# Moving tiles of a fused encoder layer by 32 bytes in SBUF

## The chip, the cores and the metric

The kernel runs on one core of a Trainium2 chip, in one launch. The metric is device microseconds of that core, from the first to the last instruction of the program; the figure that counts is the median of several runs.

## The reference

One layer of a bidirectional encoder over 512 tokens of width 2048, with 16 learned tokens put in front. All operands are float32.

```python
hn = rmsnorm(h, pre_norm_g)                       # h: 16 + 512 tokens
proj = hn @ w_in                                  # split into qa ka va ga qb kb vb gb
# mixer A: 8 query heads of 128, 2 key/value heads, norm and axial rotary on q and k
ya = softmax(qa @ ka.T / sqrt(128)) @ va * silu(ga)
# mixer B: 8 heads; two score maps of 64 with a distance penalty
a = softmax(s1 + bias) - lam * softmax(s2 + bias)
yb = rmsnorm(a @ vb, subln_g) * (1 - lambda_init) * silu(gb)
y = concat(ya, yb) @ w_out
out = h + rmsnorm(y, post_norm_g)                 # the 512 real tokens
```

## The kernel before, in words

Every large product is made on TensorE from float32r operands. Each operand is split into a high part (ScalarE, `hi`, or the activation of L154 and L179) and the rest (VectorE, `lo`, L155 and L180), and three products are accumulated in PSUM: high x high, low x high and high x low. So every logical matmul is a triple of instructions, each with its own load of the held operand ("LDWEIGHTS") and its own stream. `Lanes.mm` (L63) and `Lanes.transpose` (L66) record all of them, so their line is that of the helper; the tile names tell them apart.

Which operand is held and which is streamed differs:
- `three` (in `dense_T`, and in the first stage, a loop over 16 slices k of the width): the weights `wh`, `wl` are held, 128 columns each, and the tokens `xh[k]`, `xl[k]` are streamed. The tiles of tokens have 528 columns (16 learned, 512 real). For keys and values (`KEYS`) they are streamed in two halves of 264 columns, for queries and gates (`REAL`) as one slice of 512 columns that begins 16 columns, 64 bytes, into the tile.
- `queries_A`: the tokens are held, in slices of 128, and the weights are streamed, 512 columns.
- `dense_out` and `product(of_y(...))`: the gated heads `oh[j]`, `ol[j]` are held, in slices of 128, and the output weights are streamed, 512 columns.
- `product(of_t(...))`: sums of gated heads, `u` and `v`, are held, in slices of 128, and sums of output weights are streamed, 512 columns. `dense_out` makes the first and the fourth column block of the output; the two blocks between take seven smaller products in place of eight: two with `of_y`, two with `of_t`, one with `of_y`, two with `of_t`.
- `transpose`: the tile is held and the identity `ident` is streamed, 128 columns.

The stages: up to some 75 us the tokens are loaded and the first head's projections are made; then the eight heads of mixer B, each with its projections; from about 500 us mixer A, with its queries in two groups (`queries_A`) and a gate per head; from about 750 us the output product. The order of TensorE's work is fixed when the program is made: `lanes` runs the dense products in a loop and, after each triple, lets waiting tasks (scores, transposes, probability times values, norms) put in a few instructions of theirs when a clock that adds up nominal durations has passed their due time. Weights come through a ring of three buffers (`wp`) on the SP queue, 512 KB at a time.

Tiles take their places from pools, one after the other in the order of their first use, each rounded up to 32 bytes in a partition. The pools `cst`, `wp`, then `ap` (later `yp`) grow from the low end. The pools `xp` (tokens) and, after it is given back, `op` (gated heads) lie against the high end, which is byte 229,344 of a partition. So, in bytes of a partition before the change:
- `xp`: `xh0` begins at 161,760 = 64 x 2,527 + 32, and the 32 tiles of 2,112 bytes (64 x 33) that follow each other all begin 32 past a multiple of 64;
- `op`: `oh0` begins at 163,808 = 64 x 2,559 + 32, and the 32 tiles of 2,048 bytes likewise;
- `ident` begins at 17,824 = 64 x 278 + 32, `rB` behind it at 18,336 = 64 x 286 + 32;
- `wh`, `wl`, and the large tiles of `ap` and `yp` (among them `u`, `v`, `ph`, `pl`, `vh`, `vl`, `p`, the scores' operands) begin at multiples of 64, and `ones_r` does.

Of the kernel before, what the change touches and what calls it, by code (L numbers as in the profile page):

```python
# [10 lines left out]
F32 = mybir.dt.float32  # L11
# [6 lines left out]
P = 128  # L18
# [90 lines left out]
def kernel(ctx: ExitStack, tc: tile.TileContext, xT, xn, xm, w_s, w_t, w_q, w_o,  # L109
# [7 lines left out]
    cst = ctx.enter_context(tc.tile_pool(name="cst", bufs=1))  # L117
# [5 lines left out]
    xp = xst.enter_context(tc.tile_pool(name="xp", bufs=1, side="right"))  # L123
# [7 lines left out]
    def ctile(shape, name, dt=F32, src=None, pool=cst):  # L131
        t = pool.tile(shape, dt, name=name, tag=name, bufs=1)
        if src is not None:
            load(t, src)
        return t

    def load(out, in_):

        tc.keep_in_program_order(nc.sync.dma_start(out=out, in_=in_))
# [32 lines left out]
    nc.scalar.dma_start(out=gcol, in_=gpre)  # L172
    xh = [xp.tile([P, NT], F32R, name=f"xh{k}", tag=f"xh{k}") for k in range(KT)]
    xl = [xp.tile([P, NT], F32R, name=f"xl{k}", tag=f"xl{k}") for k in range(KT)]

    def xload(k):
        st = ap.tile([P, NT], F32, name="xs", tag="p", bufs=6)
        load(st, xT[k])
        nc.scalar.activation(xh[k], st, AF.Identity, scale=gcol[:, k:k + 1])  # L179
        nc.vector.scalar_tensor_tensor(out=xl[k], in0=st, scalar=gcol[:, k:k + 1],  # L180
                                       in1=xh[k].bitcast(F32), op0=ALU.mult, op1=ALU.subtract)
# [38 lines left out]
    for k0 in range(0, KT, 2):  # L220
        xload(k0)
        wh, wl = wload(w_s[k0 // 2], 768, load, 2 if k0 == 0 else 1)
        xload(k0 + 1)
        for k in (k0, k0 + 1):
            for i, (segs, pss) in enumerate(zip(start, first)):
                c = slice((i + 3 * (k - k0)) * P, (i + 3 * (k - k0) + 1) * P)
                for (n0, n1), ps in zip(segs, pss):
                    three(ps[:, :n1 - n0], wh[:, c], wl[:, c], k, n0, n1)
# [8 lines left out]
    def rstd(dst, ss, n, rows=P):  # L237

        nc.gpsimd.tensor_scalar(out=dst, in0=ss, scalar1=1.0 / n, scalar2=EPS,
                                op0=ALU.mult, op1=ALU.add)  # L240
        nc.gpsimd.tensor_tensor(out=dst, in0=dst, in1=mhalf[:rows, :dst.shape[1]], op=ALU.pow)  # L241
# [18 lines left out]
    nc.vector.tensor_tensor(out=rm, in0=ssm[:, 0:1], in1=ssm[:, 1:2], op=ALU.add)  # L260
    rstd(rt, rt, DM)
    rstd(rm, rm, DM, NM)
    ident = ctile([P, P], "ident", src=ident_d)
    rB = ctile([P, NT], "rB")
    dg = ap.tile([P, NT], F32, name="dg", tag="tT")
# [14 lines left out]
    sinT = ctile([P, TT, P], "sinT", src=sin_d, pool=ap)  # L280
    gqB = ctile([P, P], "gqB", src=gq, pool=ap)
    gkB = ctile([P, P], "gkB", src=gk, pool=ap)
    sgc = ctile([P, 1], "sgc", src=gsub)
    nc.vector.tensor_scalar(out=sgc, in0=sgc, scalar1=1.0 - LAMBDA_INIT, scalar2=None,
                            op0=ALU.mult)
# [19 lines left out]
    def hi(dst, src):  # L305
        nc.scalar.activation(dst, src, AF.Copy)  # L306

    def lo(dst, src, h):
        nc.vector.tensor_tensor(out=dst, in0=src, in1=h.bitcast(F32), op=ALU.subtract)  # L309
# [446 lines left out]
    op = ctx.enter_context(tc.tile_pool(name="op", bufs=1, side="right", reuse_waits="tile"))  # L756
    oh = [op.tile([P, SEQ], F32R, name=f"oh{j}", tag=f"oh{j}") for j in range(KT)]
    ol = [op.tile([P, SEQ], F32R, name=f"ol{j}", tag=f"ol{j}") for j in range(KT)]
    for j in range(0, KT - 4, 2):
        st = wp.tile([P, 1024], F32, name="os", tag="st")  # L760
        nc.sync.dma_start(out=st.rearrange("p (i q) -> p i q", i=2),
                          in_=oscr[j // 2].rearrange("i p q -> p i q"))
        for i in range(2):
            hi(oh[j + i], st[:, i * SEQ:(i + 1) * SEQ])
            lo(ol[j + i], st[:, i * SEQ:(i + 1) * SEQ], oh[j + i])
# [273 lines left out]
```

## Time and profile before

| what | value |
|---|---|
| runs | 954.44, 956.00, 956.57 us |
| median | 956.0 us |
| span of the profiled execution | 953.9 us; the page has no other time of it |
| mean granted TensorE clock | 0.990 |
| PE busy | 926.4 us, 97% |
| DVE, ACT, POOL busy | 584.6, 482.0, 164.0 us |
| data moved | 117.16 MB, mean 123 GB/s |

PE is TensorE's matmuls, PEld its loads of held operands, DVE VectorE, ACT ScalarE, POOL GpSimd, SP the engine whose queue issues most transfers. In a row of the groups stand: line, engine, operation, output <- inputs by the program's names (for a matmul the streamed operand first, then the held one: `pd<-xh,wh` streams `xh` past held `wh`), the shape, the count, the busy time and mean ns of one, and the idle time before. A matmul's recorded duration overlaps the next one's; the distance between the starts of two is what one costs. In a row of the windows stand: the stretch in us from the span's start, its length, each engine's busy time and the count of its instructions that were under way in it, the granted clock as a share of the full one, the mean share in which the transfer engines were busy, and GB/s. A row of the timeline gives start, duration, engine, line and operation; a row of the chain gives start, duration and what the end waited for.

### The profile page before, as it was taken

The numbers are of one execution on the slowest core, as the hardware profiler recorded it, in microseconds if no ns is written. First come the engines' busy times: TensorE is split into PE (matmuls) and PEld (weight loads), VectorE is DVE, ScalarE is ACT, GpSimd is POOL, SyncE is SP. The second block draws the span as 40 slices with busy tenths as digits, with TensorE's granted clock in tenths as the row PEclk, the third lists the DMA queues.
The fourth block names the chain that finished last, engine by engine and source line by source line (L and its number), as shares of the span: only waits on it lengthen the run. The fifth ranks groups of instructions, "written<-read, shape, count | busy, mean of one in ns | idle before, by whom it ended". The sixth has DMA issues, their size and how long they took to land.

```text
span 953.9 us, 14190 instructions
## 1 busy us (share of the span) xinstructions
PE 926.4 (97%) x5498; PEld 810.8 (85%) x5498; DVE 584.6 (61%) x974; ACT 482.0 (51%) x845; POOL 164.0 (17%) x250
## 2 busy tenths in 40 slices
PE   9999999999999999999999999998999999999983
PEld 8899898989989898998997888886888888888862
DVE  6386576757575574757554274447554662476996
ACT  6664655546464554746552254354555743245531
POOL 0001010101001010101201041226212123201054
PEclk9999999999999999999999999999999999999996
DMA  9742122222223222312223223211222346976785
GB/s 333 260 159 99 67 88 88 79 77 100 76 78 99 82 84 77 100 67 78 89 67 100 89 68 109 67 58 54 80 75 78 128 141 202 292 226 193 232 278 196
DMA packets 40611, 117.16 MB, mean 123 GB/s; under 512 B 4672, under 2 KB 9536, under 8 KB 40416
## 3 DMA queue, kind: packets, MB, share of 16 engines
q1 hardware_dynamic: 37072, 104.71, 33.2%
q0 software_dynamic: 3328, 11.54, 4.1%
q8 instruction: 43, 0.70, 0.3%
q14 instruction: 24, 0.20, 0.1%
q10 hardware_dynamic: 144, 0.01, 0.0%
HBM read 107.85 MB, written 8.39 MB: 122 GB/s over the span
## 4 chain that ended last, share of the span: by engine, by line
PE 84%; DVE 7%; DMA 2%; POOL 2%; ACT 2%; issue 1%; SPq 0%; DVEq 0%; POOLq 0%; ACTq 0%
PE pd L63 54%; PE po L63 14%; PE sc L63 6%; PE pv L63 5%; PE tr L66 5%; DVE wl L155 1%; DVE qn L578 1%; DMA st<-in_w_o_dram 1%; DVE y L939 1%; POOL qn L592 1%; DMA ch<-in_w_o_dram 1%; POOL ssh L241 1%; DMA xns<-in_xn_dram 1%; DMA xs<-in_xT_dram 1%; ACT qn L650 0%
## 5 line engine op out<-in xcount | busy, mean ns | idle before, releaser
L63 PE MATMUL pd<-xh,wh 128*128 128x264 f32 (+1 forms) x992 | 333.3, 336 | 0.0
L63 PE MATMUL pd<-xl,wh 128*128 128x264 f32 (+1 forms) x992 | 324.9, 327 | 0.4 <-DVE xl L180 0.4
L63 PE MATMUL pd<-xh,wl 128*128 128x264 f32 (+1 forms) x992 | 324.9, 328 | 0.4 <-DVE wl L155 0.4
L154 ACT ACTIVATE wh<-st 128x1024 fp32r<-128x1024 f32 (+2 forms) x135 | 139.8, 1038 | 208.3 <-PE pd L63 90.5
L155 DVE TENSOR_TENSOR wl<-st,wh 128x1024 fp32r<-128x1024 f32 (+2 forms) x135 | 161.7, 1198 | 98.9 <-ACT wh L154 97.7
L63 PEld LDWEIGHTS pd<-xh,wl 128*128 128x128 f32 x992 | 186.6, 188 | 17.8 <-DVE wl L155 0.7
L63 PEld LDWEIGHTS pd<-xh,wh 128*128 128x128 f32 x992 | 187.3, 189 | 12.9 <-ACT xh L179 0.2
L63 PEld LDWEIGHTS pd<-xl,wh 128*128 128x128 f32 x992 | 187.5, 189 | 12.0 <-DVE xl L180 0.6
L63 PE MATMUL po<-wh,ol 128*128 128x512 f32 x176 | 69.6, 396 | 0.9 <-DVE ol L309 0.9
L63 PE MATMUL po<-wh,oh 128*128 128x512 f32 x176 | 70.3, 400 | 0.0
L63 PE MATMUL po<-wl,oh 128*128 128x512 f32 x176 | 69.8, 397 | 0.0
L463 ACT ACTIVATE p<-p,mx 128x528 f32<-128x528 f32 x64 | 46.5, 728 | 34.2 <-POOL mx L460 34.0
L453 DVE CUSTOM_DVE_ANT_0 p<-sc,dist 128x528 f32<-128x528 f32 x64 | 44.9, 702 | 24.0 <-PE sc L63 23.5
L309 DVE TENSOR_TENSOR pl<-tr,ph 128x512 fp32r<-128x512 f32 x64 | 43.4, 688 | 16.2 <-ACT ph L306 15.0
L306 ACT ACTIVATE ph<-tr 128x512 fp32r<-128x512 f32 x64 | 37.6, 590 | 30.9 <-PE tr L66 30.6
L63 PE MATMUL pd<-wh,xh 128*128 128x512 f32 x128 | 52.2, 408 | 0.8 <-DVE vf L300 0.8
L66 PE MATMUL tr<-ident,p 128*128 128x128 f32 (+1 forms) x320 | 50.9, 273 | 1.7 <-DVE gA L558 0.9
L63 PE MATMUL pd<-wh,xl 128*128 128x512 f32 x128 | 50.6, 395 | 0.0
L63 PE MATMUL pd<-wl,xh 128*128 128x512 f32 x128 | 50.5, 395 | 0.0
L66 PEld LDWEIGHTS tr<-ident,p 128*128 128x128 f32 (+1 forms) x320 | 37.3, 132 | 13.4 <-DVE gA L558 1.6
L413 POOL TENSOR_SCALAR pm<-pm 32x256 fp32r<-32x256 f32 x32 | 20.1, 627 | 149.7 <-ACT pm L306 145.8
L460 POOL TENSOR_SCALAR mx<-mx 128x2 f32<-128x2 f32 x32 | 12.1, 377 | 196.0 <-DVE mx L453 196.0
(206 smaller groups left out, 1582.6 us busy)
## 6 DMA issues: line engine op xcount, KB each, us to landing
st<-in_w_t_dram SPq DMA_DIRECT2D x82, 512.0 KB, 3.6
st<-in_w_o_dram SPq DMA_DIRECT2D x40, 512.0 KB, 4.3
st<-in_w_q_dram SPq DMA_DIRECT2D x16, 512.0 KB, 3.6
xs<-in_xT_dram SPq DMA_DIRECT2D x16, 264.0 KB, 5.7
xns<-in_xn_dram SPq DMA_DIRECT2D x8, 512.0 KB, 5.3
ch<-in_w_o_dram POOLq DMA_DIRECT2D x8, 512.0 KB, 8.8
out_dram<-y SPq DMA_DIRECT2D x16, 256.0 KB, 2.3
os<-oscr SPq DMA_DIRECT2D x6, 512.0 KB, 3.6
```

The lines of the kernel that those rows point to most:

```text
L63: self._add(self.nc.tensor.matmul(out, lhsT, rhs, start=start, stop=stop), us)
L66: self._add(self.nc.tensor.transpose(out, in_, ident), 0.109)
L154: nc.scalar.activation(wh[:, c], st[:, c], AF.Copy)
L155: nc.vector.tensor_tensor(out=wl[:, c], in0=st[:, c], in1=wh[:, c].bitcast(F32), op=ALU.subtract)
L241: nc.gpsimd.tensor_tensor(out=dst, in0=dst, in1=mhalf[:rows, :dst.shape[1]], op=ALU.pow)
L306: nc.scalar.activation(dst, src, AF.Copy)
L309: nc.vector.tensor_tensor(out=dst, in0=src, in1=h.bitcast(F32), op=ALU.subtract)
L413: nc.gpsimd.tensor_scalar(out=pm[32:64], in0=pm[0:32].bitcast(F32), scalar1=1.0, scalar2=1.0, op0=ALU.mult, op1=ALU.mult)
L453: nc.vector.tensor_tensor_reduce(out=two(p), in0=sc[:, :, :HALF], in1=two(dist[:, w0:w0 + NT]), scale=1.0, scalar=-3.0e38, op0=ALU.add, op ...
L460: nc.gpsimd.tensor_scalar(out=mx, in0=mx, scalar1=-0.125, scalar2=1.0, op0=ALU.mult, op1=ALU.mult)
L463: nc.scalar.activation(p2[m], p2[m], AF.Exp, scale=0.125, bias=mx[:, m:m + 1], accum_out=sm[:, m:m + 1])
L578: nc.vector.scalar_tensor_tensor(out=raw[:, i, :], in0=raw[:, i, :], scalar=ss[:rows, i:i + 1], in1=g[:rows], op0=ALU.mult, op1=ALU.mult)
```

## The change

A helper `pad` takes a tile of 8 columns, 32 bytes in a partition, that nothing reads or writes. It is called four times: at the end of `xp`, at the end of `op`, ahead of `ident`, and ahead of `sgc` (behind `rB`). No instruction is added, taken away or moved in order; only addresses differ.

From the sizes: `xp` and `op` grow by 32 bytes and begin 32 bytes lower, `xh0` at 161,728 = 64 x 2,527 and `oh0` at 163,776 = 64 x 2,559, and all their tiles with them begin at multiples of 64. `ident` begins at 17,856 = 64 x 279 and `rB` at 18,368 = 64 x 287. The third pad brings what follows to 64 bytes further up than before: `wp`, `ap` and `yp` move by 64 bytes and keep their places in 64.

```diff
+    def pad(pool, name):
+
+        pool.tile([P, 8], F32, name=name, tag=name, bufs=1)
+
...
     xh = [xp.tile([P, NT], F32R, name=f"xh{k}", tag=f"xh{k}") for k in range(KT)]
     xl = [xp.tile([P, NT], F32R, name=f"xl{k}", tag=f"xl{k}") for k in range(KT)]
+    pad(xp, "xpad")
...
+    pad(cst, "ipad")
     ident = ctile([P, P], "ident", src=ident_d)
     rB = ctile([P, NT], "rB")
...
     gkB = ctile([P, P], "gkB", src=gk, pool=ap)
+    pad(cst, "spad")
     sgc = ctile([P, 1], "sgc", src=gsub)
...
     oh = [op.tile([P, SEQ], F32R, name=f"oh{j}", tag=f"oh{j}") for j in range(KT)]
     ol = [op.tile([P, SEQ], F32R, name=f"ol{j}", tag=f"ol{j}") for j in range(KT)]
+    pad(op, "opad")
```

## The prediction

> **What bounds the kernel now.** I read the page first, its engine shares and the chain that ended last.
>
> ```profile
> span 953.9 us, 14190 instructions
> PE 926.4 (97%) x5498; PEld 810.8 (85%) x5498; DVE 584.6 (61%) x974; ACT 482.0 (51%) x845; POOL 164.0 (17%) x250
> PEclk9999999999999999999999999999999999999996
> PE 84%; DVE 7%; DMA 2%; POOL 2%; ACT 2%; issue 1%; SPq 0%; DVEq 0%; POOLq 0%; ACTq 0%
> PE pd L63 54%; PE po L63 14%; PE sc L63 6%; PE pv L63 5%; PE tr L66 5%; DVE wl L155 1%; DVE qn L578 1%; DMA st<-in_w_o_dram 1%; DVE y L939 1%; POOL qn L592 1%; DMA ch<-in_w_o_dram 1%; POOL ssh L241 1%; DMA xns<-in_xn_dram 1%; DMA xs<-in_xT_dram 1%; ACT qn L650 0%
> ```
>
> TensorE sets the time: 84% of the chain is matmuls, and those that read xh, xl (pd) or oh, ol (po) are 68% of the span. Nothing is removed or added, so the only thing that can change is the pace of a matmul whose operands move. A "busy" matmul here overlaps the next one, so I don't use mean durations; I use the distance between starts. Next come the groups by shape, for the counts.
>
> ```profile
> L63 PE MATMUL pd<-xh,wh 128*128 128x264 f32 x608 | 177.1, 291 | 0.0
> L63 PE MATMUL pd<-xh,wh 128*128 128x512 f32 x384 | 156.2, 407 | 0.0
> L63 PE MATMUL po<-wh,oh 128*128 128x512 f32 x176 | 70.3, 400 | 0.0
> L63 PE MATMUL pd<-wh,xh 128*128 128x512 f32 x128 | 52.2, 408 | 0.8 <-DVE vf L300 0.8
> L66 PE MATMUL tr<-ident,p 128*128 128x128 f32 x256 | 38.5, 273 | 1.7 <-DVE gA L558 0.9 <-DVE pl L309 0.8
> L63 PE MATMUL po<-wh,uh 128*128 128x512 f32 x32 | 12.5, 391 | 0.0
> ```
>
> The first operand named is the one that streams, the second the one held in the array. Each row has two sisters (three products per tile), so 3 x (384 + 176 + 128) = 2064 matmuls of 512 columns have exactly one operand that now starts 32 bytes past a multiple of 64: the streamed xh or xl slice (1152), the held oh or ol slice (528), the held xh or xl slice (384). The 512-column matmuls on u and v in the last stage have none: both operands start at multiples of 64 today. They are the comparison that the trace offers. The windows below each hold one kind alone: the product of oh and ol with the fourth weight block, u and v, the y product between u and v (again oh, ol), and the first queries of mixer A with two gates.
>
> ```profile
> 803.20:852.43 49.23, 49.23 (x212) 1.00 0.91 279
> 878.77:898.72 19.95, 19.95 (x89) 1.00 0.61 189
> 899.19:909.69 10.50, 10.50 (x46) 1.00 0.90 305
> 517.34:573.32 55.98, 55.98 (x241) 1.00 0.27 82
> ```
>
> The count takes in the one matmul that was under way at the left edge. So the spacing is 49.23/211 = 233.3 ns with oh, 19.95/88 = 226.7 ns with u and v, 10.50/45 = 233.3 ns with oh again, and 55.98/240 = 233.3 ns with xh, at full clock in all four. The same three values of 233.3 and the one of 226.7 stand under DMA shares from 0.27 to 0.91, so DMA load doesn't make the difference; the second and third windows adjoin. The start times show that this is a steady beat, not a mean over accidents:
>
> ```profile
> 896.91 0.39 PE L63 MATMUL po<-wh,vh 128*128 128x512 f32 x1
> 897.14 0.39 PE L63 MATMUL po<-wh,vl 128*128 128x512 f32 x1
> 897.36 0.39 PE L63 MATMUL po<-wl,vh 128*128 128x512 f32 x1
> 897.59 0.39 PE L63 MATMUL po<-wh,vh 128*128 128x512 f32 x1
> ...
> 899.66 0.39 PE L63 MATMUL po<-wh,oh 128*128 128x512 f32 x1
> 899.89 0.40 PE L63 MATMUL po<-wh,ol 128*128 128x512 f32 x1
> 900.13 0.39 PE L63 MATMUL po<-wl,oh 128*128 128x512 f32 x1
> 900.36 0.39 PE L63 MATMUL po<-wh,oh 128*128 128x512 f32 x1
> ```
>
> Three products take 0.68 us with v and 0.70 us with oh. 6.6 to 6.7 ns a matmul is the price that I attach to an operand that starts off a multiple of 64; 2064 of them would be 13.8 us.
>
> **What of it is really had: the settling time.** The fast beat isn't there at once. After a wait at 913.4 the u products start again:
>
> ```profile
> 913.72:916.05 2.33, 2.33 (x12) 1.00 0.78 283
> 916.05:918.54 2.49, 2.49 (x12) 1.00 0.56 197
> 910.16:912.24 2.08, 2.08 (x11) 1.00 0.93 295
> 204.48:208.44 3.96, 3.96 (x19) 1.00 0.25 88
> 211.38:215.58 4.20, 4.20 (x21) 1.00 0.22 68
> ```
>
> The first ten starts after the wait are 2.33/10 = 233 ns apart (two in flight at the left edge), the next eleven 2.49/11 = 226.4. So even with both operands aligned about ten matmuls pass at the slow pace after a wait. After the change from oh to u at 910, without a wait, nine take 2.08 us, 231 each (the third row), before 227 comes; at the change at 877 four do. I take seven. A run of 512-column matmuls shorter than that gains nothing. The last two rows are runs in a head of mixer B: 17 matmuls in 3.96 us and 18 in 4.20, 233 each, between score and value products that break them off (the counts have those in flight at the edges).
>
> **The change part by part.**
> - xh and xl (tiles of tokens) as streamed operand, 512 columns. 96 lie in the first stage, in runs of six between 264-column ones: nothing. In mixer B 14 projections x 48 = 672: the head from 200 to 256 us has 96 in runs of 17, 18, 17 and 12 and shorter ones; less seven each the four leave 36 of 96, so 252 of 672 gain, 1.7 us. Of the gates of mixer A (384) two stand in the window at 517 and are counted there; the other 288, the queries outside that window (240) and most of the first output block (some 150) run between attention steps: of their runs, hardly longer than a dozen, I take one in eight, 85 matmuls, 0.6 us.
> - xh and xl as held operand, with those two gates: the unbroken run at 517 to 573, 240 - 7 = 233 x 6.67 = 1.6 us. The chain goes through it, and the wait for the normalised queries behind it starts from its end, so it moves along.
> - oh and ol (gated heads) as held operand, from 800 to 877 us: 329 matmuls without a break, 322 x 6.67 = 2.1 us. The 48 of the y product at 899 would save 0.3 us, but the chain has left TensorE by 902:
>
> ```profile
> 800.32:877.16 76.84, 76.84 (x330) 1.00 0.81 245
> ...
> 902.19 1.22 DVE wl L155
> ...
> 905.78 5.10 DMA ch<-in_w_o_dram
> ...
> 922.69 8.85 DMA st<-in_w_o_dram
> ```
>
>   VectorE and two weight transfers carry the last 40 us; I count those 48 at nothing. In the 49 us from 803 the transfers run at a share of 0.91, and weights that come late there could eat up to 1 us of the 2.1; that stays in the range.
> - xh and xl streamed at 264 columns (3 x 608 and 96 into sc). 264 columns are 1056 bytes, 16 and a half times 64. Today the first half of the keys starts at an odd 32 and the second at a multiple of 64; afterwards it is the other way round, so one half of each pair starts well either way. The rows are, first half, second half, first half again:
>
> ```profile
> 112.34 0.28 PE L63 MATMUL pd<-xh,wh 128*128 128x264 f32 x1
> 112.71 0.28 PE L63 MATMUL pd<-xh,wh 128*128 128x264 f32 x1
> 113.07 0.29 PE L63 MATMUL pd<-xh,wh 128*128 128x264 f32 x1
> ...
> 115.24 0.29 PE L63 MATMUL sc<-s,q 128*128 128x264 f32 x1
> ```
>
>   Three products take 0.37 and 0.36 us by turns, and the two only change places: nothing.
> - The identity as streamed operand of the transposes. Four take 0.44 us in the chain, 110 ns each, for a quarter of the columns that take 227 to 233: something other than the stream, most likely the load of the held operand, sets their pace, and that operand doesn't move relative to 64. I take nothing. From above, 6.67 ns for each of some 400 would be 2.7 us; from below a loss would need them to lie on the stream, which the aligned start excludes.
>
> ```profile
> 743.23 0.44 PE tr L66 x4
> ```
>
> - rB, and the instructions of VectorE and ScalarE that write xh, xl, oh, ol: off the chain, DVE 61% and ACT 51% busy; nothing. All tiles after the third pad move by 64 bytes, so none changes its place in 64.
>
> Sum: 1.7 + 0.6 + 1.6 + 2.1 = 6.0 us, made against the profiled 953.9 us, which is 2.1 us under the median of 956.0; I subtract it from the median: 950.0. With ten matmuls to settle it is about 5, with four 7.5.
>
> **Rivals.**
> 1. No settling cost where the run starts without a wait: all 2064 gain but the 48, 13.4 us, 942.6. For it: the switch at 877 settled in four. Against: nine at 910, ten after each wait.
> 2. Only the held operand counts. The comparison at 898 shows the held operand alone; that a streamed xh costs the same is read from 233.3 in its runs, without an aligned partner. Then the out stage (2.1) and the 144 of the window at 517 that aren't gates (0.9) remain: 953.0.
> 3. The start isn't the cause, and nothing moves: 956.0. u and v also lie in another region than oh and ol. The two products of 512 columns on ones_r, with both operands at multiples of 64, take 0.24 and 0.23 us:
>
> ```profile
> 118.62 0.40 PE L63 MATMUL ss<-sh,ones_r 128*128 128x512 f32 x1
> 118.86 0.39 PE L63 MATMUL ss<-sl,ones_r 128*128 128x512 f32 x1
> 119.09 0.28 PE L63 MATMUL pd<-xh,wh 128*128 128x264 f32 x1
> ```
>
>   I put that down to settling; it is also what a wrong cause looks like. [...]
> 4. Slower. What counts is the place in 128, not 64. Today weights and u, v start 64 past a multiple of 128; the 64 bytes of shift put them on multiples of 128, while xh and oh come to 64 past one. If the beat wants the present place, the narrow matmuls (1920 keys, 448 scores, 416 values) could each lose the same 6.67 ns: 18.6 us against the sum's 6.0, so 968.6. It decides once over 900 of the 2,784 lose it. Nothing in the trace shows such a place; nothing excludes it.
>
> [...]
>
> **How the numbers follow.** The sum 0.60; rival 1 0.10; rival 2 0.08; rival 3 0.14; rival 4 0.08. The first three are faster by over 0.2% (1.9 us, about what a measurement tells from no change): 0.78. Same 0.14, slower 0.08. The range goes from rival 1, 942.0, to 955.0, which leaves out rival 4 and most of rival 3; the likeliest case alone lies from 948.5 to 952.0, by settling times from four to ten and 1 us of late weights.
>
> **What would show it.** The products of oh and ol from 800 us at 226.7 ns a matmul; the run at 517 the same; in mixer B runs that begin at 233 and end at 227; transposes at 110 and 264-column matmuls at 121 as before; the last 50 us unchanged in length. Wrong would be: 233.3 in the unbroken runs (rival 3), 226.7 at once everywhere (rival 1), 264-column matmuls beyond 121 (rival 4), or new waits for weights in the out stage.

## The result, and the profile after

| | before | changed |
|---|---|---|
| median, runs side by side | 956.25 us (954.40 to 956.87, 10 runs) | 953.76 us (952.49 to 955.52, 10 runs) |
| ratio, with 95% interval | | 0.9981 [0.9972, 0.9990] |
| span of the profiled execution | 953.9 us | 952.0 us |
| mean granted TensorE clock | 0.990 | 0.991 |

The medians differ by 2.5 us; the ratio, 0.9981, stands for 1.8 us (1.0 to 2.7). The forecast was 6.0. Two rows of the page after the change:

```profile
span 952.0 us, 14190 instructions
PE 926.1 (97%) x5498; PEld 811.3 (85%) x5498; DVE 584.9 (61%) x974; ACT 481.6 (51%) x845; POOL 162.8 (17%) x250
```

The instructions are the same, in the same order, and TensorE is busy for 926.1 us as against 926.4. The 13.8 us that the prediction could have had at most are nowhere. The windows that answer to those of before hold oh and ol with the fourth weight block, u and v, the y product between, and the first queries of mixer A (stretch, length, then PE, PEld, DVE, ACT and POOL each with its count, then clock, DMA share, GB/s):

```profile
803.31:852.30 48.99, 48.99 (x211) 39.27 (x210) 25.05 (x33) 16.60 (x26) 9.14 (x13) 1.00 0.91 277
879.21:897.79 18.58, 18.58 (x83) 15.40 (x82) 18.58 (x19) 12.25 (x17) 3.57 (x2) 1.00 0.65 197
899.64:909.43 9.79, 9.79 (x43) 7.89 (x42) 9.52 (x11) 3.29 (x4) 0.58 (x1) 1.00 0.89 306
517.38:572.37 54.99, 54.99 (x239) 44.72 (x238) 23.38 (x37) 19.39 (x48) 10.71 (x12) 1.00 0.27 79
```

The count again takes in one matmul under way at the left edge. The spacing is 48.99/210 = 233.3 ns with oh, 18.58/82 = 226.6 with u and v, 9.79/42 = 233.1 with oh again: all as before, although oh and ol now begin at multiples of 64. The queries alone are faster, 54.99/238 = 231.1 against 233.3. The 233.3 in the unbroken runs is the sign which the prediction named as wrong. But 231.1 is no pace: it is a mixture. The queries take twelve matmuls for each token slice k, and the start times of the changed kernel's matmuls show another pace for each k:

```profile
533.09 0.39 PE L63 MATMUL pd<-wl,xh 128*128 128x512 f32 x1
...
535.38 0.39 PE L63 MATMUL pd<-wh,xh 128*128 128x512 f32 x1
...
536.08 0.39 PE L63 MATMUL pd<-wh,xh 128*128 128x512 f32 x1
...
538.12 0.40 PE L63 MATMUL pd<-wh,xh 128*128 128x512 f32 x1
...
540.68 0.39 PE L63 MATMUL pd<-wl,xh 128*128 128x512 f32 x1
```

From the first row to the second lie ten matmuls on k = 9, 2.29 us, 229.0 each. From the third to the fourth lie nine on k = 10, 2.04 us, 226.7. From the fourth to the fifth lie eleven on k = 11, 2.56 us, 232.7. All these slices start at multiples of 64. What tells them apart is their place in 256 bytes: a token tile is 2,112 bytes, 64 more than a multiple of 256, so the slice moves on by 64 from one k to the next while the weights stay. Counted as held start less streamed start, modulo 256, the distance is 192 at k = 9, 0 at k = 10, 64 at k = 11. In the out stage it is 64 for oh and 0 for u and v; before, it was 160 for oh, 0 for u and v, and an odd multiple of 32 for every token slice.

Since the order is the same (in e6 but for three), the matmuls of two traces can be matched one to one. The table shows by how much TensorE of each kernel is ahead of the kernel before; e1 to e6 are the kernels of the experiments below (us, by the start of the matmul that begins at the given time before; the last column is the span):

| kernel | 76 | 502 | 578 | 754 | 804 | 915 | last | span |
|---|---|---|---|---|---|---|---|---|
| changed | 0.0 | 0.2 | 0.6 | 1.2 | 0.6 | 0.4 | 1.2 | 1.9 |
| oh as weights (e1) | -0.1 | 0.1 | 0.5 | 0.9 | 1.0 | 3.6 | 1.0 | 2.1 |
| all at odd 32 (e3) | 0.7 | 1.2 | 1.6 | 2.7 | 2.7 | 2.9 | 3.5 | 3.4 |
| tokens as weights (e4) | 0.9 | 2.8 | 3.8 | 4.7 | 4.8 | 5.0 | 5.3 | 5.9 |
| the same, 32 off (e4c) | -0.2 | 0.2 | 0.2 | 0.6 | 0.6 | 0.6 | 1.4 | 2.1 |
| tokens and oh (e5) | 0.2 | 2.0 | 3.1 | 4.6 | 4.3 | 5.4 | 5.6 | 5.2 |
| and residual moved (e6) | 0.0 | 1.8 | 2.9 | 3.9 | 4.2 | 4.2 | 10.0 | 5.4 |

Up to 76 us the chain of the kernel before has two loads in it (`xs`, 4.79 us from 2.11, and `xns`, 4.86 from 38.25), and one execution differs from the next there by several tenths: e4 and e5 have the same addresses up to there and differ by 0.6; e2, not in the table, is 1.4 behind at 76.

### The profile page after: what moved, and what is told of

It reads as the page before. It is cut to its first block, busy times and chain, and to the rows that moved or that the text cites. A ratio compares the mean times of both kernels' runs of the same rounds, so it can differ in the third digit from the quotient of the medians.

```text
span 952.0 us, 14190 instructions
## 1 busy us (share of the span) xinstructions
PE 926.1 (97%) x5498; PEld 811.3 (85%) x5498; DVE 584.9 (61%) x974; ACT 481.6 (51%) x845; POOL 162.8 (17%) x250
## 4 chain that ended last, share of the span: by engine, by line
PE 77%; DMA 7%; DVE 7%; ACT 3%; POOL 3%; issue 2%; DVEq 0%; POOLq 0%; ACTq 0%
PE pd L63 55%; PE po L63 8%; PE sc L63 5%; PE tr L66 5%; PE pv L63 4%; DMA ts<-oscr 3%; DMA ch<-in_w_o_dram 2%; DVE qn L585 1%; DVE wl L159 1%; DVE y L947 1%; DMA st<-in_w_o_dram 1%; POOL qn L599 1%; DMA os<-oscr 1%; POOL ssh L246 1%; ACT oh L313 0%
## 5 line engine op out<-in xcount | busy, mean ns | idle before, releaser
L557 ACT ACTIVATE p<-sc,mxA 128x528 f32<-128x528 f32 x32 | 22.4, 700 | 44.6 <-POOL mxA L554 44.5
```

Source lines behind the costliest of these rows:

```text
L557: nc.scalar.activation(two(p), sc[:, :, :HALF], AF.Exp, scale=ASCALE, bias=mx, accum_out=sm)
```

## The experiments

The runs are named m1, e1 and so on; each ratio is against the kernel before, run beside that kernel. Three theories stood after this. S, the prediction's: each operand's own start in 64 bytes sets the pace. R: the region sets it (u and v lie elsewhere than oh). D: the distance between the held and the streamed start, modulo 256, sets it.

**The pair alone (m1).** A small kernel on zeros that leaves the layer out: 24 matmuls per case, held slices at a chosen distance from the streamed ones.

```
h = (m + d) // 4 + (i % 4) * P          # held: start m + d bytes, slices 512 bytes apart
s = m // 4 + (i % 2) * 1024             # streamed: start m bytes
mm(ps[:, :n], held[:, h:h + P], moved[:, s:s + n], ...)
```

> Only matmuls on zeros, none of the layer: for each case 24 matmuls that alternate over two streamed slices, with held slices at a set distance in bytes from the streamed ones. Theory D (the distance between held and streamed start, modulo 256, sets the beat; in the trace after, the queries with xh at distance 0 run at 226.7 ns, at 192 at 228.6, all others at 232 to 235): 512 columns at distance 0 and at 256 and 512 take 226 to 227 ns, whether the streamed slice starts at 0 or 32 past; 64 and 128 take 232 to 234 in both; 320 as 64. Theory S (each operand's own start in 64 bytes sets it, as predicted): all distances that are multiples of 64 run alike at 226.7 with start 0, and all cases with start 32 at 233 or more. Theory R (the region of SBUF in which the tiles lie sets it): no case differs from another of its width. For 264 and 256 columns D expects the same order of distances with 1 to 3 ns between best and worst, around 121 and 118 ns; S and R none.

Each row of the timeline is one case, named by its streamed columns, the streamed start m and the distance d. The next row's start less its own, over 24, is the spacing.

```profile
22.99 5.60 PE L36 MATMUL c512m0d0z<-moved,held 128*128 128x512 f32 x24
28.43 5.61 PE L36 MATMUL c512m0d16z<-moved,held 128*128 128x512 f32 x24
33.88 5.75 PE L36 MATMUL c512m0d32z<-moved,held 128*128 128x512 f32 x24
39.47 5.76 PE L36 MATMUL c512m0d48z<-moved,held 128*128 128x512 f32 x24
...
89.75 5.66 PE L36 MATMUL c512m0d192z<-moved,held 128*128 128x512 f32 x24
95.25 5.76 PE L36 MATMUL c512m0d208z<-moved,held 128*128 128x512 f32 x24
...
111.91 5.63 PE L36 MATMUL c512m32d0z<-moved,held 128*128 128x512 f32 x24
117.37 5.76 PE L36 MATMUL c512m32d64z<-moved,held 128*128 128x512 f32 x24
122.97 5.67 PE L36 MATMUL c512m32d192z<-moved,held 128*128 128x512 f32 x24
128.48 5.62 PE L36 MATMUL c512m0d256z<-moved,held 128*128 128x512 f32 x24
133.93 5.76 PE L36 MATMUL c512m0d320z<-moved,held 128*128 128x512 f32 x24
139.53 5.63 PE L36 MATMUL c512m0d512z<-moved,held 128*128 128x512 f32 x24
```

Distance 0 gives (28.43 - 22.99)/24 = 226.7 ns, 16 gives 227.1, 32 gives 232.9, 192 gives 229.2. With both starts moved by 32 the distances 0 and 64 give 227.5 and 233.3, and 256 and 320 give 227.1 and 233.3 like 0 and 64. Over the last twelve of each case, when the beat is steady, 0, 16, 240, 256 and 512 have 226.67, 192 has 228.9, 176 has 230.0, and all others lie between 232.1 and 234.3. Starts at an odd 32 do no harm here if both are so (227.5 at distance 0); starts at multiples of 64 don't help if they are 64 apart (232.9). S falls, and R too, since both tiles stay where they are; D stands for 512 columns. With 264 columns the steady spacing is 120.0 to 123.3; with 256 columns it is 117.1 to 120.0, and distance 0 is among the slowest, against D's expectation.

**oh and ol to the place of the weights (e1), u and v away from it (e2).** On the changed kernel; room comes from writing `lpr` in place.

```diff
-    lpr = ctile([P, 2, 64], "lpr")
+    lpr = lmt[:, 0::2, :]
+    pad(cst, "lowpad", 256)
-    pad(op, "opad")
+    pad(op, "opad", 96)          # e1
+    pad(yp, "ypad", 64)          # e2, ahead of the chain's tiles
```

> The changed kernel with the gated heads 64 bytes lower, so that held oh and ol and streamed wh and wl start at the same place modulo 256 (128 and 128); the low pools move by 256 bytes, lpr is written in place. Theory D: the unbroken products of oh and ol from 800 us on go from 233.3 to 226.7 ns a matmul, the queries and gates of mixer A stay at 231 to 232 in the mean; 329 x 6.7 = 2.2 us less by 877 us, 1.5 to 2.5 us off the changed kernel's time, so 0.995 to 0.997 of the kernel before. Theory S: both start at multiples of 64 already, 233.3 as in the changed kernel, no change against it (0.998). Theory R: oh and ol stay in the same region, 233.3, no change.

> The changed kernel with 64 bytes of padding ahead of the tiles of the output stage, so that held u and v lie 64 bytes past the streamed weights modulo 256; all still start at multiples of 64. Theory D: the products of u and v slow from 226.7 to 233.3 ns; the 94 ahead of the y product take 0.6 us more, the end 0 to 1 us later because VectorE carries it. Theories S and R: u and v stay at 226.7.

e1 took 953.40 us, a ratio of 0.9974 [0.9963, 0.9984], an interval that overlaps the changed kernel's: the 1.5 to 2.5 us that were expected don't show in the time. e2 took 954.74 in one run; it is read for its paces only, as are the other single runs (e3, e4c). The windows of e1 (oh; u and v) and of e2 (the same):

```profile
803.34:852.29 48.95, 48.95 (x217) 40.55 (x216) 26.69 (x35) 18.34 (x30) 8.71 (x12) 1.00 0.88 276
880.01:897.90 17.89, 17.89 (x80) 14.82 (x79) 17.72 (x19) 10.62 (x14) 0.00 (x0) 1.00 0.69 217
```

```profile
803.40:852.39 48.99, 48.99 (x211) 39.27 (x210) 25.16 (x34) 16.57 (x25) 9.31 (x14) 1.00 0.91 279
879.70:898.35 18.65, 18.65 (x81) 14.96 (x80) 18.65 (x19) 12.24 (x17) 3.01 (x2) 1.00 0.63 196
```

With oh at the weights' place its products take 48.95/216 = 226.6 ns; with u and v off it theirs take 18.65/80 = 233.1. Either pace was switched by addresses alone. From 804 to 877 us, where oh and ol run alone, TensorE's lead grows by 2.0 us in e1. It is 3.6 us at 915 us, and 1.0 at the last matmul. Where the rest went is in e1's timeline, TensorE, VectorE and POOL in turn:

```profile
932.91 0.80 PE L63 MATMUL po<-wl,vh 128*128 128x512 f32 x1 [7.19 <-DVE wl L159]
```

```profile
929.97 1.75 DVE L948 SCALAR_TENSOR_TENSOR y<-y,ry,xr 128x512 f32<-128x512 f32 x1 [5.36 <-POOL ry L939]
931.64 1.21 DVE L159 TENSOR_TENSOR wl<-st,wh 128x1024 fp32r<-128x1024 f32 x1
```

```profile
925.75 0.54 POOL L961 DMA_DIRECT2D xr<-in_xn_dram  x1 [3.17 <-DMA xr<-in_xn_dram]
927.22 0.54 POOL L961 DMA_DIRECT2D xr<-in_xn_dram  x1 [0.93 <-DMA xr<-in_xn_dram]
...
929.36 0.57 POOL L939 TENSOR_TENSOR ry<-ry,mhalf 128x1 f32<-128x1 f32 x1
```

TensorE waits 7.19 us for the last low part of the weights. It stands on VectorE behind a row of the output, which waits 5.36 us for the row scale; that stands on POOL behind its own loads of the residual (`xr`), two of which wait 4.1 us for earlier ones to land. The gain in the out stage became a new wait.

**Everything at an odd 32 (e3).** The kernel before, with `lpr` written in place as above and one pad of 416 bytes behind `nlam`: weights, oh, u and v all begin at 224 in every 256 bytes, and the token tiles stay at odd multiples of 32.

> The kernel before, without any of the change's padding, with the weights, u and v moved up by 160 bytes modulo 256, so that xh, oh, u, v and the weights all start 32 past a multiple of 64, and oh, ol, u, v at the same place modulo 256 as the weights (224). Theory D: oh and ol at 226.7 ns from 800 us, u and v at 226.7 as before, and among the queries one slice in four at 226.7. Theory S: every 512-column matmul has two operands that start badly: 233 or slower for oh, and u and v slow to 233 or more. Theory R: oh 233.3, u and v 226.7.

One run, 952.29 us. Its windows, oh and then u and v:

```profile
800.79:833.87 33.08, 33.08 (x147) 27.40 (x146) 14.03 (x19) 10.57 (x18) 9.51 (x14) 1.00 0.92 278
880.22:896.99 16.77, 16.77 (x75) 13.89 (x74) 16.77 (x18) 10.52 (x14) 0.17 (x1) 1.00 0.68 203
```

33.08/146 and 16.77/74 are both 226.6 ns, with no operand at a multiple of 64. That ends S in the kernel itself. Yet from 804 to 877 us TensorE's lead doesn't grow: behind this window it stands three times for a low part of the weights, `wl` (spacings of 0.89 us at 834.6, 0.95 at 840.8, 0.52 at 852.6), and these take the whole gain.

**The tokens to the place of the weights (e4), and 32 bytes beside it (e4c).** On e1's base, with oh as in the changed kernel. The pitch of 2,304 bytes is what keeps every k at one distance.

```diff
-    xh = [xp.tile([P, NT], F32R, name=f"xh{k}", tag=f"xh{k}") for k in range(KT)]
+    xh = [xp.tile([P, 576], F32R, name=f"xh{k}", tag=f"xh{k}")[:, 0:NT] for k in range(KT)]
...                                       # xl likewise
-    pad(xp, "xpad")
+    pad(xp, "xpad", 160)                 # e4; 128 in e4c
...
+                    dynamic_dma_scratch_size=10240)
```

> The changed kernel, but the 32 tiles of tokens stand 2304 bytes apart instead of 2112 and begin at 64 in every 256 bytes, so that each 512-column slice of tokens (64 bytes into its tile) and the weights begin at the same place modulo 256. Room: the descriptor buffer of POOL's transfers is 10,240 bytes instead of 16,384, lpr is written in place, pads are moved. oh and ol stay as in the changed kernel, 64 from the weights. Theory D (the distance between the starts of the held and the streamed operand, modulo 256, sets the pace): the unbroken run at 517 goes from a mean of 231.2 to 226.7 after some five to ten matmuls, 1.0 us; in mixer B, whose 512-column runs are 17 or 18 long, the first ten stay at 232 and the rest come to 227, about 1.0 us over 672; the 264-column products of keys, whose halves now stand at distances 64 and 32, go from a mean of 121.2 towards 120.0, up to 2.2 us over 1824. Together 2 to 4 us ahead of the changed kernel at 750 us, oh and ol at 233.3 as before, and about as much at the end: 950 to 952 in the median. Theory W (what TensorE saves ahead of the output stage is lost there, since the last weights come by DMA no earlier): ahead by 2 to 4 us at 750, but under 1 us at the end, 953.

> As e4, but the tiles of tokens begin at 96 in every 256 bytes: 32 bytes further up, nothing else differs. The 512-column slices of tokens then stand 224 from the weights (modulo 256), the halves of the keys 32 and 0. Theory D: the run at 517 at 233.3 throughout (slower than the 231.2 of the changed kernel, 0.5 us), the keys as in e4 at 120, mixer B's 512-column runs at 232 to 233: 2 to 3 us behind e4 at 750 us. If the pitch of 2304 or the smaller descriptor buffer made e4's gain, this one shows it too.

e4 took 951.58 us, 0.9959 [0.9945, 0.9973]; e4c 953.60 in one run. The run of queries in e4, then in e4c:

```profile
515.91:568.94 53.03, 53.03 (x235) 43.92 (x234) 23.36 (x37) 19.39 (x48) 10.44 (x12) 1.00 0.27 81
```

```profile
517.40:572.22 54.82, 54.82 (x236) 44.11 (x235) 23.41 (x37) 19.40 (x48) 9.96 (x12) 1.00 0.26 78
```

53.03/234 = 226.6 ns against 54.82/235 = 233.3, by 32 bytes and nothing else. In the table e4 is ahead of e4c by 4.2 us at 804 and by 3.9 at the last matmul: what is won ahead of the out stage stays won, and the transfers there move along: the last weight transfer on the chain begins at 916.87 us in e4 and at 920.86 in e4c. 1.1 us of the 4.2 is there by 76 us, of which the 98 products of 512 columns account for 0.5 (229.9 against 234.6 ns in the mean, with a spacing above 300 counted as 300); the rest is of the size by which executions differ there. From 76 to 502 us e4 gains 1.9: the 688 matmuls of 512 columns there take 231.8 ns in the mean against the changed kernel's 234.8 (2.1 us), while the 264-column ones take 124.0 against 123.7. The 2.2 us that the expectation allowed for the keys didn't come; between runs of other products the small kernel's steady differences don't show.

**Both (e5), and the residual's loads moved (e6).** e5 is e4 with `pad(op, "opad", 96)`. e6 is e5 with the residual of the second half in free tiles, loaded earlier:

```diff
+    xh_ = [[op.tile([P, 512], F32, name="xr", tag=f"o{'hl'[t]}{g}") for g in range(4)]
+           for t in range(2)]
+    ...                                  # the eight loads, on POOL's queue
     for u, ps in enumerate(product(of_y(1, 1), pd)):
...
-    xh_ = [[yp.tile([P, 512], F32, name="xr", tag=f"u{'hl'[t]}{g}") for g in range(4)] ...
```

> As e4, and oh and ol begin at 128 in every 256 bytes like the weights, so all 512-column products have the same place for both operands. Theory D for TensorE: oh and ol at 226.7 from 800 us, some 3 us more than e4 at 915 us. Theory W for the end: as in the run with oh alone moved, TensorE then waits some 7 us near 925 for the last weights, which stand on VectorE behind a sum that waits for the residual's loads on POOL's queue; so the end comes under 1 us before e4's: 949.5 to 951.5. If nothing were lost in the last stage, 947.

> As e5, and the eight loads of the residual's second half go into the tiles of oh and ol that are free by then, issued before the fifth of the seven smaller products instead of after the sixth (the scheduler then sets a few instructions of the last 40 us in another order). Theory W: the wait of 7 us near 925 goes or shrinks to the landing of the last weights, and 2 to 3 us of what the output stage gained reach the end: 946 to 949. Rival: the last weight transfer sets the end anyway, since it starts when a buffer comes free and takes 8 us beside the others: same as e5 within 0.7 us; or the earlier loads push weights back, and it is slower than e5.

e5 took 950.43 us, 0.9945 [0.9924, 0.9966], within its forecast, but not by the way that was expected. At 915 us its TensorE is 0.4 us ahead of e4's, not 3: oh and ol do run at 227 ns from 799 to 838 us (38.81/171), but then TensorE stands twice for `wl` (spacings of 0.78 us at 838.4 and 0.65 at 849.9). And the wait of 7 us near 925, e1's, isn't there: e5 waits 3.2 us for `wh` and 2.3 for `wl` in the last stretch, nearly as the kernel before.

e6 took 950.27, 0.9941 [0.9919, 0.9963]: the same. The forecast of 946 to 949 failed, although e6 shortens the waits. The waits of TensorE in the last stretch, in the kernel before (from 900 us) and in e6 (from 870):

```profile
PE po L63 <- ACT wh L154: 3.1, 1, 3.1
PE po L63 <- DVE wl L155: 2.2, 2, 1.1
```

```profile
PE po L63 <- DVE wl L159: 2.2, 4, 0.8
```

The last matmul in the timeline, before and in e6:

```profile
940.65 0.39 PE L63 MATMUL po<-wl,vh 128*128 128x512 f32 x1
```

```profile
930.63 0.39 PE L63 MATMUL po<-wl,vh 128*128 128x512 f32 x1
```

And some pieces of e6's chain:

```profile
924.78 2.04 POOL y L905
926.83 0.26 POOL ry L943
...
929.47 2.08 DVE y L954 x3
```

TensorE ends 10 us earlier than in the kernel before and the program 5.4 us earlier; in e5 it was 5.6 and 5.2. Part of this step is the clock. In the kernel before its granted share is 0.50 from 930.9 to 937.7 us, behind the waits, and most matmuls there start 427 ns apart; in e5 it is 0.50 from 924.9 to 931.7; in e6 it falls only at 934.0, behind TensorE's last matmul. By the chain, behind the weights come POOL's multiplication and row scale and VectorE's rows, one after the other, and they end at 948.5; in e5, where TensorE waits 5.5 us for weights in the last stretch, the end is at 948.6.

**The residual alone (e7), and POOL's multiplication on VectorE (e8).** e7 is the changed kernel with the loads moved as in e6. e8 is e6 with

```diff
-        block_done(1, 1, u)
+        block_done(1, 1, u, TTv)     # the multiplication by gpB on VectorE
```

> The changed kernel as it is, with only the residual's loads moved as in e6 (into free tiles of oh and ol, ahead of the fifth smaller product). In e6 TensorE ended 10 us earlier than in the kernel before, and the program only 5.4 us earlier. Theory V (once the residual is there, TensorE no longer waits for the last weights, but VectorE's and POOL's rows after them set the end): TensorE ends some 4 us earlier than in the changed kernel, the end moves by less than 1 us: 953 to 954. Rival (the last weights set the end, and the moved loads let them come earlier): 951 or less.

> As e6, and the two multiplications by the norm's weights that follow the sixth smaller product go from POOL to VectorE, which in e6 stands idle for 2.1 us just then, waiting for the row scales that POOL makes behind them. Theory V (VectorE and POOL carry the last 25 us): the first row scale is ready 1.4 to 2 us earlier, and the end comes 1 to 2 us earlier than e6: 948.5 to 949.5. Rival (the output transfers or the last product's own chain set the end): no gain over e6, 950.3 within 0.7 us.

e7 took 954.95 us, 0.9991 [0.9980, 1.0002]: no better than the changed kernel, though its last matmul starts at 933.24, 6.3 us earlier than there. So the loads are no gain by themselves, and the end isn't TensorE's any more. e8 took 950.54 us, 0.9944 [0.9928, 0.9959], the same as e6. Its profiled execution is 2.0 us shorter (946.5), but the median shows nothing of it: the half of V that says which instructions carry the tail is not settled.

**Fewer held columns (m2).** Again matmuls alone, on zeros: held slices of 128, 96, 64 and 32 columns at the distances 0, 64, 128, 192, 48 matmuls a case. In the last cases the distance changes by turns; the view leaves the first number out of their names, so the row of 96 holds two cases, 0 and 64 singly and in pairs.

> A kernel of matmuls alone, on zeros; it leaves the layer out. Each case has 48 matmuls of 512 streamed columns, each with its own load of a held slice; the held slices have 128, 96, 64 or 32 columns (512 to 128 bytes) and start 0, 64, 128 or 192 bytes (modulo 256) from the streamed slices; in the last cases the held slices change between distances by turns. Theory L (the reads that load the next held slice hinder the reads of the running stream, and how much depends on the distance): with 128 columns 226.7 at distance 0 and 233.3 at 64 and 128 as before; with fewer columns the excess of 6.7 shrinks with the number of columns, to about 3 with 64 and 1.7 with 32, and where the distances change by turns the slow spacing is that of the matmul under whose stream the slice of the other distance is loaded. Theory O (the distance costs something once at each matmul's begin): 6.7 of excess at every width.

The timeline's rows, named by the held columns and the distance; the next start less the own, over 48, is the spacing:

```profile
23.49 11.04 PE L34 MATMUL w128d0z<-moved,held 128*128 128x512 f32 x48
34.37 11.36 PE L34 MATMUL w128d64z<-moved,held 128*128 128x512 f32 x48
45.57 11.32 PE L34 MATMUL w128d128z<-moved,held 128*128 128x512 f32 x48
...
67.73 11.20 PE L34 MATMUL w96d0z<-moved,held 128*96 128x512 f32 x48
78.77 11.13 PE L34 MATMUL w96d64z<-moved,held 128*96 128x512 f32 x48
89.74 11.28 PE L34 MATMUL w96d128z<-moved,held 128*96 128x512 f32 x48
...
145.36 11.12 PE L34 MATMUL w64d192z<-moved,held 128*64 128x512 f32 x48
156.32 11.28 PE L34 MATMUL w32d0z<-moved,held 128*32 128x512 f32 x48
167.44 11.29 PE L34 MATMUL w32d64z<-moved,held 128*32 128x512 f32 x48
178.56 11.22 PE L34 MATMUL w32d128z<-moved,held 128*32 128x512 f32 x48
...
200.75 22.52 PE L34 MATMUL w128d_64z<-moved,held 128*128 128x512 f32 x96
223.11 11.28 PE L34 MATMUL w128d_128z<-moved,held 128*128 128x512 f32 x48
234.23 11.04 PE L34 MATMUL w64d_64z<-moved,held 128*64 128x512 f32 x48
```

With 128 columns 0 and 64 take 226.7 and 233.3. With 96 columns 64 is the faster, 228.5 against 230.0 at 0; with 64 columns 192 is the fastest, (156.32 - 145.36)/48 = 228.3; with 32 columns 0 and 64 are equal, 231.7. Neither theory holds: at distance 64 the excess over 226.7 is 6.6, 1.8, 5.8 and 5.0 ns with 128, 96, 64 and 32 columns, which neither shrinks with the load as L has it nor is the fixed cost of O. The best of the four distances is another at 128, at 96 and at 64 columns. Distances by turns don't give each matmul the pace of its own distance: with 128 columns, 0 and 64 by turns take (223.11 - 200.75)/96 = 232.9, near 64 alone, and with 64 columns they take 11.04 us for 48, as long as 128 columns at 0, that is 226.7 each, where 0 alone takes 230.0 and 64 alone 232.5. So D is shown for a distance that stays the same from one matmul to the next; what sets the pace otherwise, and why, is open.

## Why the prediction went wrong

- **The price, 6.6 to 6.7 ns.** Its size was right: e1 to e4c move long runs of 512 columns between 226.7 and 233.3, and m1 finds little between them: 228.9 at distance 192, 230.0 at 176. The step that failed is the one that attached it to "an operand that starts off a multiple of 64". The comparison behind it, oh against u, differed in two things, oh's own start (odd 32 against 64) and its distance from the weights (160 against 0), and the second decided. Rival 3's heading, "the start isn't the cause", was right; its "nothing moves" was not, since the change also moved the distances.
- **Held oh and ol, 2.1 us: nothing.** 233.3 before and after; the distance went from 160 to 64. With the distance at 0 the 2.0 us of e1 are this term: the size was right and the condition wrong.
- **Held xh and xl at 517, 1.6 us: 0.5.** (233.3 - 231.1) x 238. One slice in four comes to distance 0, one to 192; and of the twelve on k = 10 the first three take 231 each, before the nine at 226.7.
- **Streamed xh and xl in mixer B, 1.7 us: 0.2,** by which the changed kernel's lead grows from 76 to 502 us. For those after the queries, 0.6 us, it grows by 0.6 from 578 to 754, but in e1, with the same addresses, by 0.4. With the distance at 0 in e4 mixer B did give 1.9, so the size was near and the condition wrong.
- **Settling.** That a run gains only behind a settling time was right, by the three at 231 on k = 10. In e4 the runs of 17 and 18 in mixer B take 229.0 ns in the mean behind their first spacing (227.2 to 231.8 from run to run), against 232.9 in the kernel before: more than half of the price, where the prediction took 36 of 96.
- **Keys, transposes, nothing.** Right: 264-column matmuls in mixer B have a mean of 123.8 ns before and 123.7 after, and transposes one behind the other start 109.7 ns apart in both. That the load of the held operand sets the transposes' pace was the author's estimate; no run shows it.
- **"Late weights could eat up to 1 us".** Too small where oh gained at all: in e1 the last weights took back 2.6 of 3.6 us, and from 804 to 877 us the lead grew by 0.8 in e5 and not at all in e3, in place of 2.0.
- **The 2.5 us that came.** TensorE's lead at its last matmul explains 1.2. In that one pair of traces 0.6 of the lead at 754 us goes into a wait for a gate (`gA`), and the last weights return more, by a shorter wait: 2.2 us for `wh` where it was 3.1 before. So the lead is 1.9 at 930 us; then the granted clock is 0.50 in both kernels up to 937 us, more of the changed kernel's matmuls fall into that stretch, and 0.7 is lost again.

```profile
PE tr L66 <- DVE gA L565: 0.6, 1, 0.6
...
PE po L63 <- ACT wh L158: 2.2, 1, 2.2
```

  These two vary from kernel to kernel with the same addresses up to there (e1 waits 0.2 us for the gate). The 1.2 is near the 1.8 of the ratio; whether the remaining 1.3 us in the medians is more than such scatter is open.
- Rival 2's 953.0 is near the result, for another reason: oh, which it counted on, gained nothing. Rival 4 named a place in a larger unit than 64, and that was the right direction; the narrow matmuls didn't pay for it (123.8 and 123.7 ns).

In m2 the same stream past 128 held columns takes 226.7 ns with the held slice at distance 0 and 233.3 at 64, so for float32r the place of the held slice isn't without effect on the stream. That the load takes bandwidth from the stream isn't shown: at distance 64 the excess is still 5.0 ns with 32 held columns, where theory L had 1.7.

## What to carry to other kernels

Before a difference between two groups of instructions becomes a rule, list all that differs between the groups; here one small kernel that varied the two candidates separately settled in 0.2 ms what the trace couldn't. In a kernel bound by float32r matmuls of 512 streamed and 128 held columns, give the held and the streamed operand the same place modulo 256 bytes, and a pitch that keeps it for every slice: here that took each such matmul in long runs from 233.3 to 226.7 ns, some 3%, and 0.55% off this kernel (e5, 0.34 to 0.76), with no instruction added, taken away or moved. Here, what TensorE gained ahead of a stage that waits for transfers arrived at the end (e4 is 4.8 us ahead at 804 us and 5.3 at the last matmul); of what it gained within that stage little did (e1 has 3.6 at 915 us and 1.0 at the last matmul; from 804 to 877 us e3 gained nothing and e5 0.8), so look at what is late next before counting it.

## What was not expected of the hardware

- The pace of a float32r matmul (512 streamed columns, 128 held) went with the distance of the two operands' starts modulo 256 bytes: in m1 226.7 ns at 0 and 16 on either side, 228.9 at 192, 230.0 at 176, 232 to 234 elsewhere. With both starts moved by 32 bytes it was 227.5 at distance 0 and 233.3 at 64 (m1, over the whole case), and with weights, oh, u and v all at 224 in every 256 bytes 226.6 (e3).
- Which distance was best went with the held columns (m2): 0 at 128 (226.7 ns), 64 at 96 (228.5), 192 at 64 (228.3), of the four tried. With 64 held columns, 0 and 64 by turns were faster than any of the four alone: 226.7.
- The pace isn't constant within a case: at distance 64 the spacings on k = 11 of the changed kernel alternate between 231 and 236 ns, at 0, on k = 10, they come to 226 and 227. With oh, also at 64, they are 233 and 234.
